# A hybrid RWKV-7 and sparse-attention block on one core: matmuls that nobody reads, the rates in two parts, the norms read back earlier, and new interleaving tables

## The chip, the core and the metric

The kernel runs on one core of a Trainium2 chip. The metric is device time in microseconds of one execution. Engines are named as in the profile: PE is the matmul engine (PEld its weight loads), DVE the vector engine, ACT the scalar engine, POOL the general engine, SP the engine that only issues transfers. Each engine runs its own instructions in the order in which the program lists them, and waits for the others through semaphores.

## The reference

One layer for 512 tokens of width 1024. A normalised, modulated input `h` goes through one projection `w_in` of 6856 columns, which feeds two branches: an RWKV-7 recurrence (eight heads of 64) and attention over keys that an indexer selects. Both are gated, merged and projected out.

```
h = rms_norm(x, norm_w) * (1 + scale) + shift;  p = h @ w_in
w = exp(-DECAY_SCALE * sigmoid(w0 + tanh(wd) @ w_up));  a = sigmoid(a0 + ad @ a_up)
kk = k * k_k / max(norm(k * k_k), 1e-12)
state = state * w_t + (state @ -kk_t) b_t^T + v_t k_t^T;  y_t = state @ r_t
sc = relu(iq . ik);  idx_score = sum_h iw_h * sc_h;  sel = top_k(idx_score, 128)
p = softmax(q . k_sel);  y_b = p @ v_sel
out = x + gate * ((sigmoid(gm_a) * y_a @ w_a_out + sigmoid(gm_b) * y_b @ w_b_out) @ w_o)
```

## The kernel before

All matrices stay on chip in tiles of 128 partitions. Each large projection is made as three matmuls per 128 rows (the high part of one operand times both parts of the other, and the low part times the high one), so that single-precision accuracy is kept. The recurrence is done in eight chunks of 64 tokens: rates per token (`rwkv_rates`), products of keys and rates (`products`), Gram matrices per head and chunk (`gram`), a triangular solve of 32 by 32 blocks on DVE (`solve`), and the chain over the chunks (`chain`). The attention branch has the index scores (`index_pair`, for four query blocks i and four pairs of heads t), the top-128 search (`topk_ops`, alternating MAX8 and MATCH_REPLACE8 on DVE) and the attention itself.

The order of the instructions is written by hand from three generators:

- `main` emits the dependent work (front, index pairs and rates, `prep`, `solve`, eight times `chain`, `attention`), and yields after each step. The n-th yield of a pair (pe, dv) is step n.
- `projections`, the filler, emits the blocks of the big projections, 48 matmuls of 128x512 or 96 of 128x256 to a block, in the order `VRRRVRgqgkvvbbssKQssssss`. It blocks where the next block needs a buffer: the third R waits until the products of head pair 0 are done (`p0`), the first q until `p3`, the first s until the solve is done.
- `dve` holds generators of work for DVE alone: the top-128 search of query blocks 1 to 3, and the group norm.

After step n, `pull(GT[n])` takes about GT[n] us of filler, or as much as there is until it blocks, and `pull_dve(DT[n])` takes that much of `dve`. So the tables GT and DT decide where filler and search stand between the dependent steps, on PE and DVE and, through what the filler needs, on ACT and SP.

A weight half-block comes in by one SP transfer into one of three `wraw` buffers, ACT makes the high part `whi`, DVE the low part `wlo` (L255), and the transfer for the next half-block is queued behind that `wlo`.

`rwkv_rates(t)` makes two matmuls into two banks `ps_yc`, Tanh and Copy on ACT, a scan on DVE, two Exp on ACT that need the scan, a copy on DVE and, last on ACT, the Tanh of the second bank. `index_pair` makes six matmuls into two banks `ps_a` and two Relu on ACT, each followed by one multiply-add on DVE. There are two `ps_a` banks in all, so the next pair's matmuls wait for the Relus of this one.

`norms(t)` writes squared norms (`ds`) to the DRAM tensor `dD` through the ACT queue. `solve` reads them back as `db` and `dR` through the SP queue; PE transposes `dR` (L50), and DVE makes reciprocals of both and scales `PN` with `db`. `PN` itself is read back through the SP queue from `dAB`, which `gram` writes through the POOL queue; the last part of it needs `gram(3)`. After the loop of the solve, its result goes out to DRAM (`dXT`, `dX`) and comes back turned (`X1`, `TT`) before the next matmuls of `solve`.

Of the kernel before, what the change touches and what calls it, by code (L numbers as in the profile page):

```python
# [38 lines left out]
def hybrid_block_kernel(ctx, tc, x, c, norm_w, w_ada, b_ada, w_in, mu, w0, w_up, a0, a_up, k_k, k_a,  # L39
# [6 lines left out]
    def mm(*a, **k):  # L46
        return nc.tensor.matmul(*a, **k)  # L47
# [502 lines left out]
    ETA = {}  # L550

    def rwkv_rates(t):
        Et = T(f"E{t}", [128, 2, S], name="Et")
        E, ta = Et[:, 0], Et[:, 1]
        WX = T("WX", [128, NCH, 65], bufs=4)
        ps, psa = bank("yc"), bank("yc")
        mm(ps, lora[0:64, t * 128:(t + 1) * 128], wdad[0:64, :], start=True, stop=True)
        mm(psa, lora[64:128, t * 128:(t + 1) * 128], wdad[64:128, :], start=True, stop=True)
        act(E, ps, AF.Tanh, scale=0.5, bias=w0h[:, t:t + 1])
        act(E, E, AF.Copy, bias=1.0)  # L560
        L = T("sqL", [128, S], bufs=2, name="L")
        V.tensor_tensor_scan(L, smask, E, 0.0, op0=ALU.mult, op1=ALU.add)
        V.memset(WX[:, :, 0:1], 1.0)
        act(WX[:, :, 1:65], c3(L), AF.Exp, scale=-0.5 * DECAY)
        act(E, L, AF.Exp, scale=0.5 * DECAY)
        V.tensor_copy(wc[:, t, :], WX[:, :, 64])
        act(ta, psa, AF.Tanh, scale=0.5, bias=w0h[:, 4 + t:5 + t])
        ETA[t] = E, ta, WX

    KR, AK, VS, SQ = {}, {}, {}, {}  # L570

    def products(t):
        k, r = KR[t]
# [86 lines left out]
    def prep():  # L660
        for t in range(4):
            yield from need(f"kr{t}")
            yield from need(f"v{t}")
            yield gp(f"need2.{t}")
            yield from products(t)
            if t:
                yield from gram(t - 1)
            else:
                yield gp(f"prod0")
            yield from norms(t)  # L670
            yield from vtrans(t)
            bonus(t)
        V.tensor_copy(bon[64:128, 1], bonn[64:128, 0])
        V.tensor_copy(bon[0:64, 0], bonn[0:64, 1])
        QD['bon'].dma_start(bon[64:128, 0], bonn[0:64, 0])
        QD['bon'].dma_start(bon[0:64, 1], bonn[64:128, 1])
        yield from gram(3)
        done.add("prep")

# [3 lines left out]
    def solve():  # L683
# [1 line left out]
        XT = [XB[:, e] for e in range(2)]  # L685
        X1 = T("E1", [128, NQ, 32], name="X1")
        TTs.extend([T("ar", [128, 16, 64], bufs=2, name="TT") for _ in range(2)])
        db, dR = T("db", [128, 32]), T("dR", [32, 2, 64])
        dzs.append(T("dz", [128, 4, NCH]))
        dz = dzs[0].rearrange("p t c -> p (t c)")  # L690
        for s in range(2):
            QD['db'].dma_start(db[s * 64:s * 64 + 64], dD[:, s].rearrange("t c (b j) -> t (c b) j", j=32))
        for t in range(4):
            QD['db'].dma_start(dR[t * 8:t * 8 + 8], dD[t].rearrange("s c j -> c s j"))
        for e in range(2):
            G.memset(XT[e], 0.0)
            G.memset(XT[e].rearrange("p i j -> p (i j)")[:, e:512:34], 1.0)
# [603 lines left out]
            yield (*gp("need"), 0)  # L1301
        raise RuntimeError(labels)

    def main():
        yield from front()
        RATE = {(1, 1): 0, (1, 3): 1, (2, 2): 2, (3, 0): 3}
        for i in range(1, NT):
            for t in range(4):
                if (i, t) in RATE:
                    rwkv_rates(RATE[i, t])  # L1310
                    yield gp(f"rate.{RATE[i, t]}")
                index_pair(i, t)
                yield gp(f"idx.{i}.{t}")
            dve.append(topk_ops(i))
        yield from prep()
# [11 lines left out]
        yb_split()  # L1327
        done.add("main")

    GT = {0: 2.673, 1: 4.974, 2: 0, 3: 0, 4: 5.748, 5: 0, 6: 0, 7: 5.092, 8: 4.025, 9: 46352.3, 10: 10797.4, 11:  # L1330
# [15 lines left out]
    DT = {0: 0, 1: 1.2, 2: 1.2, 3: 1.2, 4: 0, 5: 0.3, 6: 0.3, 7: 0, 8: 0, 9: 0, 10: 1.5, 11: 0, 12: 0.36, 13: 0.95,  # L1346
# [12 lines left out]
    n = 0  # L1359
    for pe, dv, *w in main():  # L1360
        if w:
# [36 lines left out]
```

## Time and profile before

| | |
|---|---|
| median of three runs | 592.88 us (589.55, 592.88, 593.78) |
| profiled execution | 591.66 us, span 590.0 us |
| PE busy | 537.2 us, 91% of the span |
| DVE busy | 421.2 us, 71% |
| ACT busy | 250.4 us, 42% |
| mean granted clock of PE | 0.957 |

Busy times of matmuls overlap one another, since they are pipelined: what PE does per microsecond is read from the distance between the starts of two matmuls, not from their durations. The clock that PE is granted is either 1.00 or 0.50 in this trace; a mean between them is a mixture of both.

The stages of the span: loads and modulation to about 65 us; projections with the first index pairs to 105; index pairs and rates without filler to 133; products and Gram parts with filler to 192; the last two Gram parts to about 224; the triangular solve to 288; the chain of chunks to 366; attention to about 498; merge and output to 590.

### The profile page before, as it was taken

Reading aid. Unit: us, or ns where it says so; the run is one execution under the profiler, and the core shown is the slowest. Engines: PE = TensorE matmul, PEld = TensorE weight load, DVE = VectorE, ACT = ScalarE, POOL = GpSimd, SP = SyncE. Lnnn points to the kernel's source line nnn. Section 1 sums busy time; section 2 is a strip of 40 time slices with the busy share of each in tenths; the row PEclk is TensorE's granted clock in tenths of the full one; section 3 lists DMA queues with packets and bytes.
Section 4 is the critical chain, followed back from the end, with each engine's and each line's share of the span. In section 5 each row is a group of like instructions: output and inputs, shape, how many; then the busy total and the mean of one; then the engine's idle time right before and its main releaser. Section 6 shows DMA issues by size and latency. Waiting matters only on the chain.

```text
span 590.0 us, 10466 instructions
## 1 busy us (share of the span) xinstructions
PE 537.2 (91%) x4091; PEld 443.8 (75%) x4091; DVE 421.2 (71%) x973; ACT 250.4 (42%) x468; POOL 58.6 (10%) x100
## 2 busy tenths in 40 slices
PE   1699999569999798999789998999998999999997
PEld 0577777327877596998577777987776778998997
DVE  4796667587999665899965566866885637887442
ACT  5833564556344351532434343434535644224110
POOL 7000000002021334020010120220000000000000
PEclk9999999758999797999789999999999999999999
DMA  8992422104645594232473451313221125565522
GB/s 298 318 349 82 117 71 76 33 0 116 177 111 162 144 229 121 72 126 72 142 196 117 170 175 63 89 56 108 73 71 37 37 71 176 147 185 184 168 72 72
DMA packets 80637, 75.00 MB, mean 127 GB/s; under 512 B 15737, under 2 KB 76226, under 8 KB 80588
## 3 DMA queue, kind: packets, MB, share of 16 engines
q1 hardware_dynamic: 74492, 59.86, 34.1%
q0 software_dynamic: 3776, 12.22, 6.9%
q10 hardware_dynamic: 2320, 2.26, 1.2%
q8 instruction: 32, 0.52, 0.4%
q14 instruction: 17, 0.14, 0.1%
HBM read 62.63 MB, written 11.55 MB: 126 GB/s over the span
## 4 chain that ended last, share of the span: by engine, by line
PE 56%; DVE 28%; ACT 6%; DMA 5%; issue 4%; SPq 1%; POOL 1%; DVEq 0%; ACTq 0%
PE ps_pj L47 38%; PE ps_yc L47 6%; PE ps_a L47 5%; DVE wlo L255 4%; PE ps_z L47 3%; DVE bias L527 2%; PE ps_yc L50 2%; DVE m L525 2%; DVE sg L91 2%; PE ps_o L47 2%; DVE pt L724 1%; DVE gacc L91 1%; DMA dAB<-lx 1%; DMA x1b<-in_x_dram 1%; DVE XT L726 1%
## 5 line engine op out<-in xcount | busy, mean ns | idle before, releaser
L47 PE MATMUL ps_pj<-hh,wlo 128*128 128x512 f32 (+1 forms) x304 | 124.3, 409 | 3.7 <-DVE wlo L255 3.7
L47 PE MATMUL ps_pj<-hh,whi 128*128 128x512 f32 (+1 forms) x304 | 124.6, 411 | 1.5 <-ACT hh L88 1.0
L47 PE MATMUL ps_pj<-hl,whi 128*128 128x512 f32 (+1 forms) x304 | 124.2, 409 | 0.8 <-DVE hl L199 0.8
L255 DVE TENSOR_TENSOR wlo<-wraw,whi 128x1024 fp32r<-128x1024 f32 (+2 forms) x80 | 82.9, 1055 | 21.9 <-ACT whi L88 21.8
L88 ACT ACTIVATE whi<-wraw 128x1024 fp32r<-128x1024 f32 (+2 forms) x80 | 71.0, 921 | 25.3 <-DVE xr L1221 19.2
L47 PEld LDWEIGHTS ps_pj<-hh,wlo 128*128 128x128 f32 (+1 forms) x304 | 58.5, 192 | 17.1 <-DVE wlo L255 4.2
L47 PEld LDWEIGHTS ps_pj<-hh,whi 128*128 128x128 f32 (+1 forms) x304 | 58.7, 194 | 16.6 <-ACT hh L88 1.6
L47 PEld LDWEIGHTS ps_pj<-hl,whi 128*128 128x128 f32 (+1 forms) x304 | 58.6, 193 | 15.1 <-DVE hl L199 1.6
L47 PE MATMUL ps_pj<-whi,hh 128*128 128x256 f32 x192 | 54.8, 286 | 0.0
L47 PE MATMUL ps_pj<-whi,hl 128*128 128x256 f32 x192 | 54.4, 283 | 0.0
L47 PE MATMUL ps_pj<-wlo,hh 128*128 128x256 f32 x192 | 54.3, 283 | 0.0
L47 PEld LDWEIGHTS ps_pj<-whi,hh 128*128 128x128 f32 x192 | 36.4, 189 | 0.6
L47 PE MATMUL ps_pj<-whi,mh 128*128 128x256 f32 x128 | 36.4, 284 | 0.0
L47 PEld LDWEIGHTS ps_pj<-whi,hl 128*128 128x128 f32 x192 | 36.2, 189 | 0.0
L47 PEld LDWEIGHTS ps_pj<-wlo,hh 128*128 128x128 f32 x192 | 36.1, 188 | 0.0
L47 PE MATMUL ps_pj<-whi,ml 128*128 128x256 f32 x128 | 36.0, 281 | 0.0
L47 PE MATMUL ps_pj<-wlo,mh 128*128 128x256 f32 x128 | 36.0, 281 | 0.0
L525 DVE MAX8 m<-bias 128x8 f32<-128x256 f32 (+2 forms) x48 | 26.8, 558 | 1.1
L527 DVE MATCH_REPLACE8 bias<-m,bias 128x256 f32<-128x256 f32 (+2 forms) x48 | 26.1, 543 | 0.0
L47 PEld LDWEIGHTS ps_pj<-whi,mh 128*128 128x128 f32 x128 | 24.1, 188 | 0.2 <-ACT gate L88 0.2
L47 PEld LDWEIGHTS ps_pj<-wlo,mh 128*128 128x128 f32 x128 | 24.1, 188 | 0.2 <-issue 0.2
L47 PEld LDWEIGHTS ps_pj<-whi,ml 128*128 128x128 f32 x128 | 24.1, 188 | 0.0
(312 smaller groups left out, 1043.1 us busy)
## 6 DMA issues: line engine op xcount, KB each, us to landing
wraw<-in_w_in_dram SPq DMA_DIRECT2D x44, 512.0 KB
wa<-in_w_ada_dram SPq DMA_DIRECT2D x32, 256.0 KB
lxc<-dLX POOLq DMA_DIRECT2D x8, 768.0 KB, 5.2
wraw<-in_w_in_dram SPq DMA_DIRECT2D x18, 256.0 KB
dLX<-lx SPq DMA_DIRECT2D x8, 512.0 KB
wraw<-in_w_ada_dram SPq DMA_DIRECT2D x8, 512.0 KB
wraw<-in_w_o_dram SPq DMA_DIRECT2D x8, 512.0 KB
wraw<-in_w_a_out_dram SPq DMA_DIRECT2D x16, 128.0 KB
```

The costliest lines, as they stand in the source:

```text
L47: return nc.tensor.matmul(*a, **k)
L50: return nc.tensor.transpose(*a, **k)
L88: A.activation(o, i, func, **kw)
L91: V.scalar_tensor_tensor(o, a, s, b, op0=op0, op1=op1, **kw)
L255: eng.tensor_sub(l_, r_, f(h_))
L525: V.max(out=m8, in_=acc)
L527: V.match_replace(out=acc, in_to_replace=m8, in_values=acc, imm_value=MARK)
L724: V.tensor_mul(pv[e], XT[e][:, a0:, j + 1:], PN[:, j, None, j + 1:].to_broadcast([128, m, n]))
L726: V.tensor_reduce(XT[e][:, (j + 2 - e) // 2:, j], pv[e], axis=AX.X, op=ALU.add)
```

## The change

It has four parts.

1. `warm(count)` emits matmuls of one and the same pair of 128x128 and 128x512 tiles of `hh` into the bank `ps_o`, whose result nothing reads. The table `WT` places 36 of them behind eight steps: 2 behind step 7 (the last index pair of block 1, where filler still runs), 4 behind step 11 (index pair 2.2), 5, 2 and 2 behind 14, 15 and 16 (index pairs 3.0, 3.1, 3.2), 7 behind 20 (the products of head pair 0), 9 behind 40 (first half of the Gram part of head pair 2) and 5 behind 130 (keys of the last head pair in attention). The old `main` becomes `stages`.
2. `rwkv_rates` is a generator. Its first part ends before the two Exp, and the Tanh of the second bank moves into it. The index pair that follows is emitted between the two parts.
3. `db` and `dR` are allocated and read back in `prep`, ahead of `gram(3)`, no longer in `solve`.
4. GT and DT have new values throughout.

```diff
     def rwkv_rates(t):
...
         act(E, E, AF.Copy, bias=1.0)
+        act(ta, psa, AF.Tanh, scale=0.5, bias=w0h[:, 4 + t:5 + t])
         L = T("sqL", [128, S], bufs=2, name="L")
         V.tensor_tensor_scan(L, smask, E, 0.0, op0=ALU.mult, op1=ALU.add)
         V.memset(WX[:, :, 0:1], 1.0)
+        yield
         act(WX[:, :, 1:65], c3(L), AF.Exp, scale=-0.5 * DECAY)
         act(E, L, AF.Exp, scale=0.5 * DECAY)
         V.tensor_copy(wc[:, t, :], WX[:, :, 64])
-        act(ta, psa, AF.Tanh, scale=0.5, bias=w0h[:, 4 + t:5 + t])
         ETA[t] = E, ta, WX
+        yield
...
         QD['bon'].dma_start(bon[0:64, 1], bonn[64:128, 0])
+        dbs.extend([T("db", [128, 32]), T("dR", [32, 2, 64])])
+        for s in range(2):
+            QD['db'].dma_start(dbs[0][s * 64:s * 64 + 64], dD[:, s].rearrange("t c (b j) -> t (c b) j", j=32))
+        for t in range(4):
+            QD['db'].dma_start(dbs[1][t * 8:t * 8 + 8], dD[t].rearrange("s c j -> c s j"))
         yield from gram(3)
...
-        db, dR = T("db", [128, 32]), T("dR", [32, 2, 64])
+        db, dR = dbs
...
-        for s in range(2):
-            QD['db'].dma_start(db[s * 64:s * 64 + 64], dD[:, s].rearrange("t c (b j) -> t (c b) j", j=32))
-        for t in range(4):
-            QD['db'].dma_start(dR[t * 8:t * 8 + 8], dD[t].rearrange("s c j -> c s j"))
...
+    def warm(n):
+
+        if n:
+            ps = bank("o")
+            for _ in range(n):
+                mm(ps, hh[:, 0, 0:128], hh[:, 0, :], start=True, stop=True)
+
     def main():
+        n = 0
+        for y in stages():
+            yield y
+            if len(y) == 2:
+                warm(WT.get(n, 0))
+                n += 1
+
+    WT = {7: 2, 11: 4, 14: 5, 15: 2, 16: 2, 20: 7, 40: 9, 130: 5}
+
+    def stages():
         yield from front()
         RATE = {(1, 1): 0, (1, 3): 1, (2, 2): 2, (3, 0): 3}
         for i in range(1, NT):
             for t in range(4):
-                if (i, t) in RATE:
-                    rwkv_rates(RATE[i, t])
+                rate = rwkv_rates(RATE[i, t]) if (i, t) in RATE else None
+                if rate:
+                    next(rate)
                     yield gp(f"rate.{RATE[i, t]}")
                 index_pair(i, t)
+                if rate:
+                    next(rate)
                 yield gp(f"idx.{i}.{t}")
...
-    GT = {0: 2.673, 1: 4.974, 2: 0, 3: 0, 4: 5.748, 5: 0, 6: 0, 7: 5.092, 8: 4.025, 9: 46352.3, 10: 10797.4, 11:
+    GT = {0: 4.59, 1: 4.327, 2: 0, 3: 0, 4: 13.305, 5: 0, 6: 0, 7: 5.279, 8: 1.036, 9: 148203, 10: 142844, 11:
...
```

How the rows move is shown at two places. The first is the stage of index pairs and rates that has no filler, and there first ACT, before: `Et` and `WX` are tiles of the rates, `L` the result of the scan, `rl` the Relu of an index pair.

```order
L88 ACTIVATE Et_970<-ps_yc_972,w0h_587 128x512
L88 ACTIVATE Et_970<-Et_970 128x512
L88 ACTIVATE WX_971<-L_978 128x8x64
L88 ACTIVATE Et_970<-L_978 128x512
L88 ACTIVATE Et_970<-ps_yc_973,w0h_587 128x512
L88 ACTIVATE rl_1001<-ps_a_993 128x384
L88 ACTIVATE rl_1004<-ps_a_994 128x384
```

And now, at the same place of ACT:

```order
L88 ACTIVATE Et_976<-ps_yc_978,w0h_587 128x512
L88 ACTIVATE Et_976<-Et_976 128x512
L88 ACTIVATE Et_976<-ps_yc_979,w0h_587 128x512
L88 ACTIVATE rl_996<-ps_a_988 128x384
L88 ACTIVATE rl_999<-ps_a_989 128x384
L88 ACTIVATE WX_977<-L_985 128x8x64
L88 ACTIVATE Et_976<-L_985 128x512
```

The two Relus, which the next pair's matmuls wait for, stand ahead of the two Exp that need the scan, no longer behind them. On PE the same stage before, from the matmuls of rate 2 (`lora`) to the norms (`sel`):

```order
L47 MATMUL ps_yc<-wdad,lora 128x512 x2
L47 MATMUL ps_a<-ik,iqs 128x384 x12
L47 MATMUL ps_yc<-wdad,lora 128x512 x2
L47 MATMUL ps_a<-ik,iqs 128x512 x24
L47 MATMUL ps_z<-sq,sel 2x512
```

And now, from the first index pair of that stage to the last:

```order
L47 MATMUL ps_a<-ik,iqs 128x384 x6
L47 MATMUL ps_o<-hh 128x512 x4
L47 MATMUL ps_a<-ik,iqs 128x384 x6
L47 MATMUL ps_yc<-wdad,lora 128x512 x2
L47 MATMUL ps_a<-ik,iqs 128x512 x6
L47 MATMUL ps_o<-hh 128x512 x5
L47 MATMUL ps_a<-ik,iqs 128x512 x6
L47 MATMUL ps_o<-hh 128x512 x2
```

The matmuls into `ps_o` are the unread ones; each group stands ahead of the next index pair, whose matmuls wait for Relus. The second place is the last Gram part and the start of the solve. SP before, from the last transfers of the Gram matrices:

```order
L647 DMA dLX_612<-lx_1826 128x8x128
L656 DMA PN_614<-dAB1_609 8x32x32 x4
L692 DMA db_1964<-dD_613 64x1x32 x2
L694 DMA dR_1965<-dD_613 8x2x64 x4
L321 DMA wraw_1988<-in_w_in_dram 128x4x256
```

And now, from the end of the transfers of the bonus:

```order
L679 DMA bon_621<-bonn_620 64x16
L682 DMA db_1860<-dD_613 64x1x32 x2
L684 DMA dR_1861<-dD_613 8x2x64 x4
L321 DMA wraw_1945<-in_w_in_dram 128x4x256
L321 DMA wraw_2002<-in_w_in_dram 128x4x256
L650 DMA dLX_612<-lx_1868 128x8x128
L650 DMA dLX_612<-lx_1869 128x8x128
L659 DMA PN_614<-dAB1_609 8x32x32 x4
```

The reads of `db` and `dR` were queued behind the last read of `PN`, which waits for `gram(3)`; now they stand ahead of one weight load that was ahead of them, of a second one, of the two stores `dLX` of `gram(3)`, and of that read. DVE before, from the copies of the bonus to the second half of the last Gram part (`lx`; `bias` and `m` are the top-128 search):

```order
L674 COPY bon<-bonn 64x16
L640 TENSOR_TENSOR lx<-ps_yc,mask_167 128x4x2x64
L640 TENSOR_TENSOR lx<-ps_yc,mask_167 128x4x128
L255 TENSOR_TENSOR wlo<-wraw,whi 128x2x2x64 x4
L640 TENSOR_TENSOR lx<-ps_yc,mask_167 128x4x2x64
L640 TENSOR_TENSOR lx<-ps_yc,mask_167 128x4x128
```

And now:

```order
L677 COPY bon<-bonn 64x16
L527 MATCH_REPLACE bias_1040<-m_1848,bias_1040 128x512
L525 MAX m_1891<-bias_1040 128x8
L527 MATCH_REPLACE bias_1040<-m_1891,bias_1040 128x512
L525 MAX m_1894<-bias_1040 128x8
L643 TENSOR_TENSOR lx<-ps_yc,mask_167 128x4x2x64
L643 TENSOR_TENSOR lx<-ps_yc,mask_167 128x4x128
L255 TENSOR_TENSOR wlo<-wraw,whi 128x2x2x64 x4
L527 MATCH_REPLACE bias_1040<-m_1894,bias_1040 128x512
L525 MAX m_1958<-bias_1040 128x8
L527 MATCH_REPLACE bias_1040<-m_1958,bias_1040 128x512
L525 MAX m_1961<-bias_1040 128x8
```

Eight steps of the search stand around the first half of that Gram part. Between the scaling of `PN` and the last step of the solve there were nine such steps on DVE, and now there is none.

More of the change, by code (lines that the diff above doesn't have):

```diff
@@ L566, in rwkv_rates @@
         V.tensor_copy(wc[:, t, :], WX[:, :, 64])
-        act(ta, psa, AF.Tanh, scale=0.5, bias=w0h[:, 4 + t:5 + t])
         ETA[t] = E, ta, WX
-    KR, AK, VS, SQ = {}, {}, {}, {}
+        yield
+    KR, AK, VS, SQ, dbs = {}, {}, {}, {}, []
     def products(t):
@@ L1328, in main @@
         done.add("main")
-    GT = {0: 2.673, 1: 4.974, 2: 0, 3: 0, 4: 5.748, 5: 0, 6: 0, 7: 5.092, 8: 4.025, 9: 46352.3, 10: 10797.4, 11:
[15 rows of a table removed]
-    DT = {0: 0, 1: 1.2, 2: 1.2, 3: 1.2, 4: 0, 5: 0.3, 6: 0.3, 7: 0, 8: 0, 9: 0, 10: 1.5, 11: 0, 12: 0.36, 13: 0.95,
[12 rows of a table removed]
+    GT = {0: 4.59, 1: 4.327, 2: 0, 3: 0, 4: 13.305, 5: 0, 6: 0, 7: 5.279, 8: 1.036, 9: 148203, 10: 142844, 11:
[14 rows of a table added]
+    DT = {0: 2, 1: 0.3, 2: 0, 3: 0.52, 4: 0.08, 5: 0.6, 6: 0.22, 7: 0, 8: 0.38, 9: 0.47, 10: 0, 11: 0, 12: 0.68, 13:
[12 rows of a table added]
     n = 0
```

53 rows, old and new, of tables (DT, GT) are left out of this document.

## Prediction

> **What bounds the kernel now.** I read the page first, then the granted clock over the span, the waits of PE, and the stages in which both come together.
>
> The page gives the span and, in 40 slices of 14.75 us, the clock of PE:
>
> ```profile
> span 590.0 us, 10466 instructions
> ...
> PEclk9999999758999797999789999999999999999999
> ```
>
> The profiled execution took 591.66 us, 1.66 more than its span. The dips stand between slices 8 and 22. With windows on their edges, the columns are length, then busy time of PE, PEld, DVE, ACT and POOL, then clock:
>
> ```profile
> 110.07:130.55 20.48, 13.93 (x52) 7.51 (x52) 17.40 (x42) 12.01 (x22) 0.00 (x0) 0.50 0.00 0
> 133.97:137.38 3.41, 3.41 (x23) 2.39 (x23) 3.20 (x5) 2.56 (x4) 0.00 (x0) 0.50 0.21 49
> 195.41:202.23 6.82, 5.12 (x32) 3.09 (x34) 5.51 (x12) 1.88 (x4) 1.84 (x3) 0.50 0.20 59
> 226.13:232.95 6.82, 5.91 (x14) 4.64 (x15) 4.65 (x9) 1.90 (x3) 2.77 (x5) 0.50 0.51 160
> 287.57:294.39 6.82, 5.54 (x15) 4.47 (x16) 5.64 (x9) 5.75 (x8) 0.00 (x0) 0.50 0.66 211
> 304.63:311.46 6.83, 6.39 (x135) 5.77 (x136) 3.73 (x8) 3.82 (x8) 0.00 (x0) 0.50 0.61 175
> ```
>
> In these six stretches PE works at half speed: its 40.3 busy us there hold some 20 us of work at full clock. What half speed costs is seen in the distance between the starts of two filler matmuls, 0.24 us at full clock and 0.43 at half:
>
> ```profile
> 94.87 0.40 PE L47 MATMUL ps_pj<-hh,wlo 128*128 128x512 f32 x1
> 95.11 0.40 PE L47 MATMUL ps_pj<-hl,whi 128*128 128x512 f32 x1
> ...
> 229.55 0.63 PE L47 MATMUL ps_pj<-hh,wlo 128*128 128x512 f32 x1
> 229.98 0.63 PE L47 MATMUL ps_pj<-hl,whi 128*128 128x512 f32 x1
> ```
>
> Each dip follows or holds a wait of PE. Of the list of waits (total, times, longest) these lie behind the loads:
>
> ```profile
> PE ps_a L47 <- ACT rl L88: 8.2, 4, 4.3
> ...
> PE ps_pj L47 <- DVE wlo L255: 3.7, 1, 3.7
> ...
> PE ps_yc L47 <- DVE lx L640: 3.6, 1, 3.6
> ...
> PE ps_z L47 <- ACT sq L88: 1.4, 1, 1.4
> ```
>
> Four stages, in windows again:
>
> ```profile
> 105.42:132.57 27.15, 15.65 (x63) 8.37 (x62) 21.57 (x49) 15.98 (x28) 0.49 (x1) 0.62 0.00 0
> ...
> 228.40:287.65 59.25, 56.73 (x377) 51.99 (x375) 53.94 (x136) 18.48 (x33) 4.39 (x7) 0.96 0.31 97
> 287.65:301.03 13.38, 12.18 (x48) 9.81 (x48) 8.86 (x13) 7.88 (x12) 1.63 (x3) 0.75 0.68 208
> 366.00:498.00 132.00, 129.56 (x842) 104.44 (x841) 93.35 (x262) 65.86 (x157) 6.62 (x8) 1.00 0.25 74
> ```
>
> The first is the stage of rates and index pairs without filler: nobody is full, a chain over PE, ACT and DVE sets the pace. In the solve both PE (56.73 of 59.25) and DVE (53.94) are nearly full. Attention is PE's, at full clock.
>
> **The change part by part.** *Rates in two parts.* In the first stage ACT and PE do this:
>
> ```profile
> 107.30 0.63 ACT L88 ACTIVATE Et<-Et 128x512 f32<-128x512 f32 x1
> ...
> 110.28 0.67 ACT L88 ACTIVATE Et<-ps_yc,w0h 128x512 f32<-128x512 f32 x1
> 110.85 0.86 ACT L88 ACTIVATE rl<-ps_a 128x384 f32<-128x384 f32 x2
> ...
> 118.77 1.07 ACT L88 ACTIVATE rl<-ps_a 128x512 f32<-128x512 f32 x2
> ```
>
> ```profile
> 95.67 0.80 PE L47 MATMUL ps_a<-ik,iqs 64*128 64x384 f32 x6
> ...
> 119.41 2.13 PE L47 MATMUL ps_a<-ik,iqs 64*128 64x512 f32 x6 [3.34 <-ACT rl L88]
> ...
> 121.81 2.13 PE L47 MATMUL ps_a<-ik,iqs 64*128 64x512 f32 x6 [0.27 <-ACT rl L88]
> ```
>
> After Copy (ends 107.93) ACT waits for the scan, makes two Exp and a Tanh, and only then the Relus at 110.85 that let PE go on. Now Tanh follows Copy at once and the Relus come at 107.93 + 0.67 = 108.60, 2.25 us earlier. The second round (Relus at 118.77) has the same form: 4.5 us in all. The Exp move into the time of DVE's multiply-adds.
>
> *Unread matmuls, 20 in this stage.* If they keep the clock, a pair of 512 columns takes about 0.80 x 512/384 = 1.07 us (an estimate from the 384-column row) rather than 2.13, and the distance of pairs falls from 121.81 - 119.41 = 2.40 to some 1.5, where DVE takes over: three such distances, 2.7 us. At full clock the 20 cost 20 x 0.24 = 4.8 us, in a stage in which PE had 27.15 - 15.65 = 11.5 idle. That cover gone, they cost up to 20 x 0.43 = 8.6.
>
> *Search steps in this stage.* DVE sets a floor. It is busy 21.57 us; the new order has 9 search steps here, formerly 14, each about 0.46 us (MAX8 0.425, the replacement with its load 0.49):
>
> ```profile
> L525 DVE MAX8 m<-bias 128x8 f32<-128x256 f32 x8 | 3.4, 425 | 0.1
> L527 DVE MATCH_REPLACE8 bias<-m,bias 128x256 f32<-128x256 f32 x8 | 3.3, 408 | 0.0
> ...
> L527 DVE MATCH_VALUE_LOAD bias<-m,bias 128x8 f32 x8 | 0.7, 83 | 0.2
> ```
>
> That takes 2.3 off; but index pairs 2.0 and 2.1 now stand closer to the stage, and I put 1.2 us of their multiply-adds into it. Floor 20.5, so of 4.5 + 2.7 at most 6.7 can come. Between 2 (clock not kept, one of the two advances eaten by DVE) and 6.7 I take **5.0**, near the floor, since the floor is what is busy in the row. Step 7's two matmuls stand among filler: **+0.5**.
>
> *Clock at the filler's return.* The stretch 133.97:137.38 is 3.41 busy us at half clock; the 7 matmuls behind step 20 fill the wait before it: **-1.7**, or nothing.
>
> *Nine matmuls in the wait of 3.6 us.* 9 x 0.24 = 2.2 fit in it. If the clock stays, the 5.12 busy us of 195.41:202.23 become 2.6. *Norms read back earlier.* The solve's start, by SP, PE and DVE:
>
> ```profile
> 221.80 1.36 SPq L656 DMA_DIRECT2D PN<-dAB  x2
> ...
> 223.21 1.11 SPq L692 DMA_DIRECT2D db<-dD  x2
> ...
> 224.37 1.50 SPq L694 DMA_DIRECT2D dR<-dD  x4
> ...
> 227.04 0.28 PE L50 MATMUL ps_z<-ident,dR 32*128 32x32 f32 x1 [2.91 <-DMA dR<-dD]
> ...
> 228.40 1.67 DVE L708 TENSOR_TENSOR PN<-PN,db 128x1024 f32<-128x1024 f32 x1
> ```
>
> `dR` is issued only behind `PN`. Ahead of it, its six issues take 1.1 + 1.5 us on SP while the last Gram part is being made; behind them wait one weight load and two stores that have time until the chain. So PE's 2.9 us go, and with them the dip 226.13:232.95, half of 5.91 = 3.0. What is late next is `PN`: issued to 223.16, it can be on chip at about 225 to 226, if `gram(3)` is as early as before. It is not: eight search steps stand around its first half, four of them behind it. They cost 8 x 0.72 = 5.8 us, with rows from the solve's window:
>
> ```profile
> L527 DVE MATCH_REPLACE8 bias<-m,bias 128x512 f32<-128x512 f32 x5 | 3.4, 678 | 0.0
> L525 DVE MAX8 m<-bias 128x8 f32<-128x512 f32 x4 | 2.8, 688 | 0.0
> ```
>
> DVE had idle time there, waiting for `lx` buffers:
>
> ```profile
> 206.01 0.69 DVE L640 TENSOR_TENSOR lx<-ps_yc,mask 128x512 f32<-128x512 f32 x1 [1.92 <-DMA dLX<-lx]
> ...
> 208.86 0.69 DVE L640 TENSOR_TENSOR lx<-ps_yc,mask 128x512 f32<-128x512 f32 x1 [2.16 <-DMA dLX<-lx]
> ```
>
> That covers 4.1 of the 5.8, so `PN` comes 1 to 2 us later, and DVE starts the solve at about 227 instead of 228.4.
>
> *The solve.* Its nine search steps (3.4 + 2.8, with five loads 6.6 us) are gone. DVE keeps 53.94 - 6.6 = 47.3 busy us; with its old idle time, 59.25 - 53.94 = 5.3, it is 52.6. The end moves from 287.65 to between 274.3 and 279.6; PE, which must do the same filler, has lost 2.6 + 2.9 + 3.0 us less before it and can be there at about 278. The 3.7 us wait for `wlo` behind the solve and the dip 287.57:294.39 (half of 5.54) go only in part, since the result's way through DRAM sets that stretch. For everything from 192 to 301 I take **-10**; bounds -2 (search steps come back in front of `PN`, clock lost) and -15 (2.6 + 2.9 + 3.0 + 3.7 + 2.8).
>
> *Chain, attention, merge.* Filler is the same in amount, spread otherwise. In attention PE idles 132.00 - 129.56 = 2.4 us in all, so little can be won; five matmuls stand there where filler is blocked: 0 to 2.2 us. The tables may open or close waits of 2 us. I take **+1**.
>
> Sum: 591.66 + 0.5 - 5.0 - 1.7 - 10 + 1 = 576.5. The median of the three runs, 592.88, is 1.2 above the profiled execution: **577.7**.
>
> **The rivals.**
>
> *DVE takes the gain back.* DVE is nearly full in the solve, and the work taken out is put in front of `PN`. If the idle time doesn't cover it, the solve starts 5.8 us later than the 227 above and PE waits for `wlo` again: the stretch yields about 2 instead of 10, and the time is 585.7. For: 53.94 of 59.25. Against: the two waits for `dLX` of 4.1 us.
>
> *The clock falls all the same.* The clock is low through 110.07:130.55 although PE is busy 13.93 of 20.48, so light work doesn't bring it back; the unread matmuls last 1 us at a time, and the last dip began with this wait only:
>
> ```profile
> 305.07 3.62 PE L47 MATMUL ps_yc<-TT,ZT 32*32 32x32 f32 x128 [1.83 <-DVE ZT L759]
> ```
>
> Then pairs stay at 2.13, the first stage gives 2.5, the return nothing, and the rest 8: 592.88 + 0.5 - 2.5 - 8 + 1 = 583.9. The Trainium skill, "TensorE: Matmul & The Clock Gate", in the table of "Why this matters for your kernels", asks only that no idle gap between bursts is longer than about 3 us; by that rule each group would save the clock, and the sum would stay as above. The row of 1.83 us idle behind 32x32 matmuls speaks against so simple a rule. The same page, Part 1, has the clock return only after about 3.4 us of sustained work; the stretch from 110.07 agrees.
>
> *Slower: the unread matmuls stand in the way.* At half clock five of them last 2.1 us and two 0.9, ahead of index pairs that waited only 0.27 us in the loop of 2.40. That is 1.9 + 2 x 0.6, and 7 x 0.43 - 1.4 = 1.6 from the seven ahead of the norms (the wait for `sq` in the list); with 2.2 in attention and 0.5 at step 7 it is 7.4 us. If in addition the gain of the solve is taken back and ACT's is eaten by DVE, the kernel comes to 592.88 + 7.4 - 2 = 598. It decides when a group lasts longer than the wait it stands in, which needs the low clock.
>
> **How the numbers follow.** The forecast has 0.60, DVE's return 0.18, the falling clock 0.15, the slower case 0.07. The forecast's own bounds are 592.88 + 0.5 - 6.7 - 1.7 - 15 = 570 and 592.88 + 0.5 - 2 - 4 + 2 = 589; the two middle rivals lie inside. The range goes from 569 to 589, the lower end 1 us further out for what the floor of DVE leaves open; it leaves out the slower case and the outer parts of the others. The runs of the kernel before span 0.7%, so 1% (5.9 us) is about what a measurement can tell from no change. Faster than 587 are nearly all of the forecast and most of the two rivals: 0.80; within 1%: 0.14; slower: 0.06.
>
> **What would show it.** Right: the clock at 1.00 from the filler's end to its return; the Relus of the index pair right behind the second Tanh; no wait of PE for `dR`; the stage from the first rate matmuls to the last product 22 us instead of 27; DVE's solve near 50 us instead of 59. Wrong: a dip of the clock in the stage without filler; `PN` scaled later than 228 less the earlier gains; PE waiting for `wlo` in the solve; more than 2.4 us idle on PE in attention.

## The result, and the profile after

The changed kernel takes 573.7 us in the median of its runs, the kernel before 592.9: the ratio is 0.968, with a 95% interval of 0.962 to 0.975. A second series of runs, beside other kernels, gave 573.5 us and 0.969 (0.966 to 0.972). Ratios are of fast runs; of all the kernels below only one, "search out", had a slow one among its five (578.5 us). The prediction, 577.7 with a range of 569 to 589, holds the time. Not all of its reasons hold.

The page of the profiled execution (570.04 us) has these two lines for the span and the clock in 40 slices:

```profile
span 568.3 us, 10555 instructions
...
PEclk9999999998999999999989999999999999999999
```

Two dips are left, in slices 10 and 21. Next, the span by stages, of before and then of after. A window begins with the first rate matmul behind which the filler stands still; the next edges are the filler's return, its last matmul before the Gram parts of head pairs 2 and 3, the scaling of `PN` on DVE, the end of the filler behind the solve, the filler's return at the end of the chain, and the end of the filler in attention. The six stages are called stage A, Gram 0, 1 (the products and the first two Gram parts), Gram 2, 3, the solve, the chain and attention. The columns are length, then busy time of PE, PEld, DVE, ACT and POOL, then clock.

```profile
105.42:133.60 28.18, 16.53 (x71) 9.28 (x71) 22.40 (x51) 16.91 (x30) 0.94 (x1) 0.64 0.00 0
133.60:191.93 58.33, 57.80 (x344) 44.72 (x345) 53.55 (x116) 27.36 (x45) 10.91 (x15) 0.97 0.52 144
191.93:228.40 36.47, 29.87 (x246) 25.29 (x246) 22.72 (x59) 13.65 (x30) 15.91 (x28) 0.88 0.64 165
228.40:300.23 71.83, 68.11 (x418) 61.17 (x417) 62.80 (x147) 25.63 (x42) 6.02 (x10) 0.92 0.37 114
300.23:361.89 61.66, 56.63 (x1102) 46.45 (x1100) 36.07 (x76) 23.94 (x50) 6.40 (x12) 0.94 0.50 158
361.89:493.26 131.37, 128.93 (x845) 104.02 (x844) 94.22 (x280) 65.78 (x161) 6.62 (x8) 1.00 0.22 67
```

```profile
105.71:128.11 22.40, 17.23 (x91) 9.47 (x91) 20.80 (x47) 16.59 (x30) 0.93 (x1) 1.00 0.00 1
128.11:185.81 57.70, 57.62 (x344) 44.73 (x345) 53.84 (x116) 27.98 (x46) 10.88 (x15) 0.97 0.54 150
185.81:219.34 33.53, 32.30 (x267) 27.38 (x267) 27.67 (x72) 13.97 (x30) 13.73 (x24) 1.00 0.69 179
219.34:282.02 62.68, 61.11 (x410) 56.01 (x409) 57.93 (x133) 24.91 (x41) 9.98 (x13) 1.00 0.41 129
282.02:342.70 60.68, 56.36 (x1099) 45.71 (x1096) 38.63 (x83) 23.89 (x50) 6.38 (x12) 0.97 0.50 159
342.70:471.12 128.42, 128.11 (x850) 103.69 (x849) 93.63 (x280) 66.58 (x160) 7.50 (x8) 1.00 0.23 71
```

So stage A gave 5.8 us, Gram 2, 3 gave 2.9, the solve 9.2 and attention 3.0; Gram 0, 1 and the chain gave 0.6 and 1.0. What lies ahead of stage A and behind attention became 0.3 and 0.4 us longer. In stage A the clock is 1.00 instead of 0.64, and DVE is busy 20.80 of 22.40 us.

In the list of waits of PE (total, times, longest) the waits for `dR` and for `wlo` are gone, those for `rl` and `lx` fell from 8.2 and 3.6, and the one for `kr` at the end of stage A grew from 2.1:

```profile
PE ps_z L47 <- DVE kr L91: 3.3, 1, 3.3
...
PE ps_a L47 <- ACT rl L88: 1.1, 2, 0.8
...
PE ps_yc L47 <- DVE lx L643: 0.7, 2, 0.5
```

On ACT, in order of time, the Relus of the index pair follow the second Tanh, which follows the Copy, and the two Exp come behind them. The first Relu starts 108.70 - 107.59 = 1.11 us after the start of the Copy, before it was 110.85 - 107.30 = 3.55:

```profile
107.59 0.63 ACT L88 ACTIVATE Et<-Et 128x512 f32<-128x512 f32 x1
108.13 0.67 ACT L88 ACTIVATE Et<-ps_yc,w0h 128x512 f32<-128x512 f32 x1
108.70 0.86 ACT L88 ACTIVATE rl<-ps_a 128x384 f32<-128x384 f32 x2
109.62 0.63 ACT L88 ACTIVATE WX<-L 128x512 f32<-128x512 f32 x1
```

At the start of the solve DVE now waits for what stood next in the prediction's chain, `PN`:

```profile
216.22 0.35 DVE L711 RECIPROCAL db<-db 128x32 f32<-128x32 f32 x1
219.34 1.23 DVE L712 TENSOR_TENSOR PN<-PN,db 128x1024 f32<-128x1024 f32 x1 [2.77 <-DMA PN<-dAB]
```

### The profile page after: what moved, and what is told of

It reads as the page before. It is cut to its first block, busy times and chain, and to the rows that moved or that the text cites. A ratio compares the mean times of both kernels' runs of the same rounds, so it can differ in the third digit from the quotient of the medians.

```text
span 568.3 us, 10555 instructions
## 1 busy us (share of the span) xinstructions
PE 533.4 (94%) x4127; PEld 441.3 (78%) x4127; DVE 421.2 (74%) x973; ACT 251.3 (44%) x468; POOL 61.7 (11%) x100
## 4 chain that ended last, share of the span: by engine, by line
PE 73%; DVE 15%; ACT 4%; issue 3%; DMA 3%; SPq 2%; DVEq 0%; ACTq 0%
PE ps_pj L47 54%; PE ps_yc L47 5%; PE ps_a L47 5%; PE ps_z L47 4%; PE ps_yc L50 2%; PE ps_o L47 2%; DVE sg L91 2%; DVE bias L527 2%; DVE bias L91 1%; DVE gacc L91 1%; DVE wlo L255 1%; DMA x1b<-in_x_dram 1%; DVE m L525 1%; PE ps_a L50 1%; SPq L659 1%
## 5 line engine op out<-in xcount | busy, mean ns | idle before, releaser
L47 PE MATMUL ps_pj<-hh,whi 128*128 128x512 f32 (+1 forms) x304 | 123.1, 407 | 1.0 <-ACT hh L88 1.0
L47 PE MATMUL ps_pj<-hl,whi 128*128 128x512 f32 (+1 forms) x304 | 122.4, 403 | 0.7 <-DVE hl L199 0.7
L47 PE MATMUL ps_pj<-hh,wlo 128*128 128x512 f32 (+1 forms) x304 | 122.2, 402 | 0.0
L47 PEld LDWEIGHTS ps_pj<-hh,whi 128*128 128x128 f32 (+1 forms) x304 | 57.5, 189 | 14.4 <-ACT hh L88 1.3
L47 PEld LDWEIGHTS ps_pj<-hh,wlo 128*128 128x128 f32 (+1 forms) x304 | 57.6, 190 | 12.5 <-issue 0.2
```

## The experiments

Each run was timed beside the kernel before; the ratio is to that. "Unread" are the matmuls that nobody reads. Each kernel also has a profile, cut at the edges named above; here A begins with the end of the last filler matmul, 0.1 us later. All lengths are in us; "low" is the time between the first loads and the last 2 us for which the granted clock was 0.50.

| kernel | ratio (95%) | A | Gram 0, 1 | Gram 2, 3 | solve | chain | attention | low |
|---|---|---|---|---|---|---|---|---|
| before | 1 | 28.12 | 58.33 | 36.46 | 71.83 | 61.67 | 131.37 | 51.2 |
| changed | 0.968 (0.962 to 0.975) | 22.33 | 57.70 | 33.53 | 62.68 | 60.68 | 128.42 | 6.8 |
| changed, again | 0.969 (0.966 to 0.972) | 23.13 | 58.45 | 34.39 | 63.86 | 64.68 | 128.46 | 20.5 |
| no unread | 0.970 (0.966 to 0.974) | 22.35 | 57.68 | 35.30 | 62.54 | 61.88 | 129.90 | 34.1 |
| unread late | 0.968 (0.965 to 0.971) | 22.37 | 57.70 | 33.94 | 64.17 | 62.21 | 128.43 | 27.3 |
| rates whole | 0.980 (0.976 to 0.984) | 28.81 | 57.73 | 36.34 | 62.48 | 63.71 | 128.43 | 30.7 |
| norms late | 0.976 (0.973 to 0.979) | 22.34 | 57.71 | 36.70 | 66.24 | 63.87 | 128.40 | 20.5 |
| search back | 0.980 (0.976 to 0.984) | 22.37 | 57.68 | 32.48 | 65.15 | 64.26 | 131.68 | 10.2 |
| search back, 2 | 0.971 (0.968 to 0.973) | 22.35 | 57.71 | 32.67 | 65.20 | 62.39 | 128.42 | 13.7 |
| old tables | 0.990 (0.986 to 0.993) | 26.21 | 59.09 | 33.27 | 68.97 | 62.73 | 131.37 | 30.7 |
| tables only | 0.989 (0.987 to 0.992) | 30.17 | 58.39 | 38.01 | 65.68 | 60.65 | 129.95 | 44.4 |
| kr early | 0.970 (0.967 to 0.973) | 22.37 | 57.69 | 34.42 | 63.77 | 62.32 | 128.41 | 13.7 |
| search out | 0.964 (0.961 to 0.966) | 20.93 | 58.05 | 35.23 | 64.02 | 59.20 | 128.42 | 6.8 |
| search out, late | 0.969 (0.966 to 0.972) | 23.10 | 58.82 | 33.98 | 63.95 | 62.08 | 128.41 | 34.1 |

The changed kernel itself was run again, as the mark for the runs that followed:

> The changed kernel itself, timed again beside the next three as their mark: 572 to 575, ratio 0.964 to 0.970.

It came as expected. Its two profiles show how far one profile carries: 0.1 us in attention, 0.8 in A, 2.0 in the sum of Gram 2, 3 and the solve, 4.0 in the chain. The 0.8 in A are all at its end: the last matmuls of the norms start 21.51 us behind the first rate matmul both times, and in the second profile they ran at half clock.

**Without the unread matmuls.**

```diff
-    WT = {7: 2, 11: 4, 14: 5, 15: 2, 16: 2, 20: 7, 40: 9, 130: 5}
+    WT = {}
```

> The changed kernel without its 36 unread matmuls; the rest as it is. Stage A is the stage of rates and index pairs from the filler's stop to its return: 28.1 us before, 22.4 changed. If the unread matmuls keep the clock (the forecast), the clock falls to 0.50 within some 4 us of the filler's stop, a pair of 512 columns takes about 2.1 us again, stage A is 25 to 26 us (the earlier Relus stay), a second dip comes at the Gram part of head pair 2, and the time is 578 to 583. If the tables and the split rates did it all (rival), stage A stays within 1 us of 22.4 or gets shorter and the time is 571 to 575.

The ratio is 0.970, against 0.968 and 0.969 with them. The forecast's theory had the clock right, though the fall came 9.0 us after the filler's end (104.52) and not within 4, and the time wrong. The window of stage A, and the pairs in it by time on PE:

```profile
104.45:126.87 22.42, 14.76 (x72) 7.38 (x71) 20.82 (x47) 16.47 (x30) 0.94 (x1) 0.77 0.01 1
113.53:123.77 10.24, 7.89 (x35) 3.34 (x31) 9.45 (x21) 6.27 (x11) 0.00 (x0) 0.50 0.00 0
```

```profile
115.08 2.13 PE L47 MATMUL ps_a<-ik,iqs 64*128 64x512 f32 x6 [0.72 <-ACT rl L88]
117.48 2.13 PE L47 MATMUL ps_a<-ik,iqs 64*128 64x512 f32 x6 [0.27 <-ACT rl L88]
120.97 1.87 PE L47 MATMUL ps_z<-sq,sel 128*2 128x512 f32 x2 [1.36 <-ACT sq L88]
```

The clock falls for 10.24 us and a pair takes 2.13 us again, as forecast, and the stage is as long as before within 0.02 us. DVE is busy 20.82 of it, as it was with them. The half clock lies wholly beside DVE's work.

The other places: without the nine, Gram 2, 3 is 0.9 to 1.8 us longer, but the solve behind it makes that good (35.30 + 62.54 = 97.84, between 96.21 and 98.25 of the changed kernel). Without the five, attention is 1.5 us longer, with a clock of 0.50 from 434 to 438 us, which begins 2 us behind a wait of PE of 1.2 us for `qs`; the five stand in that wait.

**Only the unread matmuls of the later places.**

```diff
-    WT = {7: 2, 11: 4, 14: 5, 15: 2, 16: 2, 20: 7, 40: 9, 130: 5}
+    WT = {40: 9, 130: 5}
```

> The changed kernel with 14 of the 36 unread matmuls: the nine at the Gram part of head pair 2 and the five in attention stay, the 22 in and ahead of stage A go. New theory: DVE sets stage A, so the clock may fall there at no cost: stage A 22.4 us within 0.5 at a clock near 0.6, the time that of the changed kernel within 1.5 us. Rival: the clock of stage A is worth the forecast's 2.7 us once the rest is in step: stage A 24 us or more, 575 to 578.

A is 22.37 us, the ratio 0.968. The 22 unread matmuls in and ahead of stage A are worth nothing there. Nor do they always keep the clock: with all of them it fell in stage A in the two kernels below that have the rates whole (111.69 to 118.52 us) or the old tables (112.72 to 119.54), at waits of PE for Relus of 4.0 and 1.7 us.

**The rates in one piece.**

```diff
         act(E, E, AF.Copy, bias=1.0)
-        act(ta, psa, AF.Tanh, scale=0.5, bias=w0h[:, 4 + t:5 + t])
...
-        yield
         act(WX[:, :, 1:65], c3(L), AF.Exp, scale=-0.5 * DECAY)
         act(E, L, AF.Exp, scale=0.5 * DECAY)
         V.tensor_copy(wc[:, t, :], WX[:, :, 64])
+        act(ta, psa, AF.Tanh, scale=0.5, bias=w0h[:, 4 + t:5 + t])
...
-                if rate:
-                    next(rate)
```

> The changed kernel with the rates in one piece again: the Relus stand behind the scan, the two Exp and the second Tanh. Forecast's term: they come 2.25 us later in each of two rounds, stage A is 25 to 27 us instead of 22.4, the time 576 to 579. Rival: DVE sets stage A (20.8 us busy of 22.4), and the later Relus cost less than 1 us: 573 to 575.

A is 28.81 us, 6.5 more, longer than either theory had it, and the time is 581.3 us, the ratio 0.980: (0.980 - 0.969) x 592 = 6.5 us. In the list of waits PE's wait for `rl` is back:

```profile
PE ps_a L47 <- ACT rl L88: 5.6, 2, 4.0
```

And the window of stage A:

```profile
106.28:135.17 28.89, 20.09 (x92) 12.09 (x91) 22.10 (x50) 16.81 (x30) 0.93 (x1) 0.82 0.01 2
```

DVE is busy 22.10 of 28.89 us: it stands still for lack of Relus and of what the Exp make. The clock is 0.82, so the 6.5 us may hold a part that the clock lost; no run separates it. Without the split, the tables and the unread matmuls bring nothing in stage A.

**The norms read back in the solve.**

```diff
-        dbs.extend([T("db", [128, 32]), T("dR", [32, 2, 64])])
-        for s in range(2):
-            QD['db'].dma_start(dbs[0][s * 64:s * 64 + 64], dD[:, s].rearrange("t c (b j) -> t (c b) j", j=32))
...
         yield from gram(3)
...
-        db, dR = dbs
+        db, dR = T("db", [128, 32]), T("dR", [32, 2, 64])
...
+        for s in range(2):
+            QD['db'].dma_start(db[s * 64:s * 64 + 64], dD[:, s].rearrange("t c (b j) -> t (c b) j", j=32))
...
```

> The changed kernel with db and dR read back in the solve again, behind PN on SP's queue. Forecast's term: PE waits some 2.9 us for dR and loses up to 3.0 more to the clock: 577 to 580. Rival: PN, not dR, lets DVE start the solve, and PE makes up the wait in the filler of the solve: less than 1 us, 573 to 575.

The median is 578.9 us, as expected; the ratio is 0.976, 0.007 x 592 = 4 us more. The wait for `dR` is back and twice as long as in the kernel before:

```profile
PE ps_z L50 <- DMA dR<-dD: 5.8, 1, 5.8
```

Gram 2, 3 and the solve together are 102.94 us against 96.21 and 98.25: 4.7 to 6.7. The forecast's 5.9 lies in that.

**Eight search steps back into the solve, twice.**

```diff
     DT = {
...
-        44: 3.07, 45: 2.33,
+        44: 0, 45: 0,
...
-        49: 0, 50: 0, 61: 0, 63: 0, 64: 0, 66: 0, 69: 0, 72: 0, 73: 0,
+        49: 0.82, 50: 0.21, 61: 1.33, 63: 0.22, 64: 0.22, 66: 0.61, 69: 0.43, 72: 0.22, 73: 1,
...
```

The first time the remainder that DVE's table carries from step to step was 0.14 us off behind the solve, so that DVE's steps stood otherwise in the chain and in attention. The second time `84: 1.06` instead of 1.2 put that right.

> The changed kernel with eight search steps of 512 columns taken from the first half of gram(3) and put back into the loop of the solve. Forecast's term: they cost 8 x 0.72 = 5.8 us on DVE in a solve in which DVE has hardly any slack; some 1 to 2 us come back at the start of the solve, which is then earlier: the stretch from the scaling of PN to the end of the filler behind the solve grows from 62.7 to 66 to 68 us, the time is 576 to 579. Rival: PE's filler sets the end of the solve and DVE's steps fit beside it: 572 to 575.

> The eight search steps back in the loop of the solve, as in the first such run, but with one table value 0.14 lower so that DVE's order from the chain on is that of the changed kernel again. If the attention's 3.3 us longer stage in the first run came from the shifted order there, it is gone (128.4 us), and what is left is the price of the steps in the solve: 575 to 579. Rival: the steps in the solve cost all of the 7.5: attention 131 us or more, 580 to 582.

The medians are 581.0 and 574.9 us, the ratios 0.980 and 0.971. With the order behind the solve the same as in the changed kernel, the eight steps in the solve cost 0.971 - 0.969, some 1 us, and the intervals overlap. Gram 2, 3 got shorter, the solve longer, and their sum is 32.67 + 65.20 = 97.87 us, between the 96.21 and 98.25 of the changed kernel. The forecast had them at 2.5 to 5.5 us of time.

The other 5 us of the first run went with the shifted order. Attention shows 3.3 of them, 131.68 instead of 128.42 us, with two waits of PE in it that the changed kernel doesn't have; where the rest went the profiles don't settle:

```profile
PE ps_yc L50 <- DVE qn L914: 1.8, 1, 1.8
PE ps_pj L47 <- ACT sq L88: 1.1, 1, 1.1
```

**The parts without the tables, and the tables without the parts.** The first kernel is the changed one with GT and DT of before, the second the one before with the new GT and DT. The edit of the first, against the changed kernel, is below; the second makes the same edit to the kernel before, the other way round:

```diff
-    GT = {0: 4.59, 1: 4.327, 2: 0, 3: 0, 4: 13.305,
+    GT = {0: 2.673, 1: 4.974, 2: 0, 3: 0, 4: 5.748,
...
-    DT = {0: 2, 1: 0.3, 2: 0, 3: 0.52, 4: 0.08,
+    DT = {0: 0, 1: 1.2, 2: 1.2, 3: 1.2, 4: 0,
...
```

> The changed kernel with the GT and DT of the kernel before, so the unread matmuls, the rates in two parts and the early norms alone. By the forecast's sum the code parts bring 5 in stage A and 5.9 of dR with its dip, less what PN still holds up, and the solve keeps its nine search steps (71.8 us to the end of the filler behind it): 580 to 584. Rival one: without the tables the parts bring little, since the search steps of the old order stand elsewhere: 587 or more. Rival two: the tables bring nothing: 573 to 576.

> The kernel before with the new GT and DT alone: rates in one piece, norms read back in the solve, no unread matmul. If the parts add up as they came off the changed kernel (7.8 for the rates, 5.4 for the norms, 0 to 1 for the unread matmuls), 573.5 + 13 to 14 = 586 to 588, so the tables alone bring 5 where they brought 12.5 on top of the other parts. Rival: tables and parts are independent, and the tables alone bring the 12.5 that were missing without them: 578 to 581. Second rival: written for the other order, they bring nothing or cost: 590 or more.

The medians are 586.0 us and 585.0 us: the parts alone bring less than the forecast's sum for them (580 to 584), the tables alone a little more than what the sum of the parts left for them. In ratios, the parts alone bring 1.0%, 6 us, the tables alone 1.1%, 6.5 us, both together 3.1%, 18 us. Their waits of PE, first of the parts without the tables, then of the tables without the parts:

```profile
PE ps_pj L47 <- DVE wlo L255: 4.4, 1, 4.4
...
PE ps_a L47 <- ACT rl L88: 2.4, 2, 1.7
```

```profile
PE ps_a L47 <- ACT rl L88: 9.7, 4, 5.5
PE ps_z L50 <- DMA dR<-dD: 5.9, 1, 5.9
```

Without the tables the wait for `wlo` stays, and the solve has 68.97 us; without the parts the waits for `rl` and `dR` get longer than they were (8.2 and 2.9). So each half runs into waits that the other half takes away. That this makes up the 18 - 12.5 = 5.5 us is a reading of the lists; no run was made to test it. Attention is 131.37 with the old tables, with the five unread matmuls and without, 129.95 with the new ones and 128.4 with the new ones and the five.

**Five search steps from behind steps 19 to 21 to behind steps 24 and 26.**

```diff
     DT = {
...
-        19: 0.6, 20: 0.6, 21: 0.5, 24: 0, 26: 0.5,
+        19: 0, 20: 0, 21: 0, 24: 1, 26: 1.2,
...
```

> The changed kernel with the five search steps behind steps 19 to 21, which stand on DVE ahead of the normalised keys that PE waits for at the end of stage A, put behind steps 24 and 26, where filler runs. If DVE sets stage A, it shortens by 1.5 to 2.3 us (five steps of 0.45 to 0.49) to about 20.3, the wait for kr falls from 3.4 to about 1.3 us, and the time falls by 1 to 2.3 us unless DVE is late with wlo in the stage behind, where it is busy 53.8 of 57.7 us. Rival: ACT or PE sets the end of stage A: no change, within 0.7 us.

A is 22.37 us, the time 574.7: no change. The expectation was wrong on the place: in DVE's row of the changed kernel these steps follow the multiply-add that writes `kr`, they do not lead it:

```profile
126.33 0.75 DVE L91 SCALAR_TENSOR_TENSOR kr<-ar,P,kb 128x512 f32<-128x512 f32 x1
127.00 0.08 DVE L527 MATCH_VALUE_LOAD bias<-m,bias 128x8 f32 x1
```

So this run says nothing on what DVE does to stage A; the next two do.

**Seven search instructions out of stage A, with and without the unread matmuls there.** The first also has six unread matmuls between the two halves of the solve's result; the second has the same DT, and of the unread matmuls only the 14 of the later places (`{40: 9, 130: 5}`).

```diff
-    WT = {7: 2, 11: 4, 14: 5, 15: 2, 16: 2, 20: 7, 40: 9, 130: 5}
+    WT = {7: 2, 11: 4, 14: 5, 15: 2, 16: 2, 20: 7, 40: 9, 130: 5, 84: 6}
...
     DT = {
...
-        12: 0.68, 14: 0.3, 15: 1.04, 16: 0.6, 24: 0, 26: 0.5,
+        12: 0, 14: 0, 15: 0, 16: 0, 24: 1.2, 26: 1.9,
...
```

> The changed kernel with the seven search instructions (four MAX8, three replacements) that stand on DVE between the index pairs of stage A, ahead of the normalised keys, moved behind steps 24 and 26, and six unread matmuls more behind the first half of the solve's result, where PE waits 1.6 us and a dip of the clock follows. If DVE sets stage A: 4 x 0.43 + 3 x 0.49 = 3.2 us less on DVE, stage A 19.2 to 20.5 us instead of 22.35. If the six keep the clock at the start of the chain, that stage stays at or below 60.7 us, where five of six profiles of the changed kernel and its kin had 61.9 to 64.7. Together 568 to 571. Rival: PE or ACT sets stage A as soon as DVE is lighter: 21.5 or more there, 572 to 574.

> The same move of the seven search instructions, with only the unread matmuls at the Gram part of head pair 2 and in attention (14). With DVE lighter in stage A the low clock may be felt there: pairs of 512 columns 2.40 apart, stage A 20.5 to 22.4 us against 19.2 to 20.5 with the unread matmuls, and 570 to 573. Rival: DVE still hides the clock, stage A equal within 0.4 us with and without them.

Stage A in windows, first with the unread matmuls, then without:

```profile
105.97:126.97 21.00, 17.06 (x92) 9.47 (x91) 18.33 (x36) 16.37 (x30) 0.94 (x1) 1.00 0.00 1
```

```profile
105.36:128.53 23.17, 16.64 (x72) 9.11 (x71) 19.09 (x38) 17.28 (x32) 0.93 (x1) 0.61 0.04 9
```

With both the search away and the clock kept, A is 20.93 us, 1.4 less than in the changed kernel (the expectation's 19.2 to 20.5 was too low); with the search away alone it is 23.10 (20.5 to 22.4 was expected), no better than in the changed kernel, and the time is 573.3 us. The pairs show why: 2.40 us apart at the half clock, 2.04 and 2.01 at the full one. At the half clock DVE, now lighter, waits for the Relus of every pair:

```profile
113.52 2.13 PE L47 MATMUL ps_a<-ik,iqs 64*128 64x512 f32 x6 [0.66 <-ACT rl L88]
115.92 2.13 PE L47 MATMUL ps_a<-ik,iqs 64*128 64x512 f32 x6 [0.27 <-ACT rl L88]
...
118.30 1.61 DVE L91 SCALAR_TENSOR_TENSOR bias<-rl,iw,bias 128x512 f32<-128x512 f32 x2 [0.79 <-ACT rl L88]
```

```profile
114.14 1.44 PE L47 MATMUL ps_a<-ik,iqs 64*128 64x512 f32 x6
115.52 0.73 PE L47 MATMUL ps_o<-hh 128*128 128x512 f32 x2
116.18 1.42 PE L47 MATMUL ps_a<-ik,iqs 64*128 64x512 f32 x6
...
118.19 1.32 PE L47 MATMUL ps_a<-ik,iqs 64*128 64x512 f32 x6
```

Two limits of nearly the same length lie beside each other in this stage: DVE with the search steps, and PE with its Relus at half clock. The norms' matmul behind the last pair starts 16.5 us after the first rate matmul under either limit (122.22 - 105.71 in the changed kernel, 121.81 - 105.36 = 16.45 without search and unread matmuls) and 15.3 when both are lifted (121.25 - 105.97). The multiply-add that writes `kr`, which the end of the stage waits for, ends 21.4 and 21.3 us behind the first rate matmul under one limit, and 20.0 when both are lifted. Lifting one shows nothing. The 0.8 us by which 23.10 is longer than 22.33 lie behind `kr`, as in the second profile of the changed kernel: the norms' last matmuls at half clock.

The six unread matmuls in the solve's result stand in the wait for `ZT`, of 1.6 us; the clock stays at 1.00 there, and the chain has 59.20 us, the least of all profiles. The first kernel's ratio, 0.964 (0.961 to 0.966), is the best of all: (0.969 - 0.964) x 592 = 3 us less than the changed kernel's second series, which ran beside other kernels, and the intervals touch. How the 3 us divide between stage A and the chain, the single profiles do not settle.

## Why the prediction was right or wrong

- **The sum.** 577.7 was forecast, 573.7 measured. The profiled execution went from 591.66 to 570.04, by 21.6 where the sum had 15.2. Stretch by stretch, with the forecast's term behind: +0.3 ahead of stage A (+0.5), -5.8 in stage A (-5.0), -0.6 at the filler's return (-1.7), -12.1 from Gram 2, 3 to the end of the solve (-10), -3.5 behind it (+1). The median fell by 19.2 only, since the profiled execution is the fastest of its four; that the forecast came within 4.0 is in part luck, as some terms are right for reasons that the runs don't bear out. The upper bound of 589 takes off 2 and 4, where the two bounds that the text names are 2 and 2: with them it is 591.
- **Rates in two parts.** Right in mechanism: the Relus come right behind the second Tanh. The term was 4.5 for ACT, with 2.7 more for the clock and a floor of 20.5 by DVE. Measured: the split is worth 6.5 us with the new tables, a lost clock included; with the old ones the split and the unread matmuls together give 1.9 (26.21 against 28.12). There DVE has 14 search instructions ahead of `kr`, in the changed kernel nine, as counted in the forecast. The floor was sized well: DVE is busy 20.80.
- **Unread matmuls in stage A.** With them the clock stayed at 1.00 in stage A in the changed kernel's first profile and up to its last 2 us in the second, as forecast, and that is worth nothing. The step "if they keep the clock ... three such distances, 2.7 us" fails, because the half clock lay beside DVE. The prediction took 5.0 of 7.2 for this very floor, but cut the sum and not the term. With DVE lighter the clock is worth 2.2 us (23.10 against 20.93), 0.8 of them in the norms' last matmuls. The term was mis-sized too: a pair of 512 columns lasts 1.3 to 1.45 us at full clock, where 384 columns gave an estimate of 1.07, and the pairs are 2.0 us apart, not 1.5, with the clock kept and the search away.
- **Clock at the filler's return, -1.7, or nothing.** It was nothing. The seven matmuls stand ahead of the norms; the wait behind them, for `kr`, was 2.1 us and is now 3.35, and the dip stayed:

```profile
128.23:131.64 3.41, 3.41 (x14) 2.28 (x15) 3.20 (x10) 2.26 (x4) 0.00 (x0) 0.50 0.29 66
```

- **Nine matmuls in the wait of 3.6 us.** The dip went, as forecast, and came back in the kernel without them. The 2.6 us show as 0.9 to 1.8 in Gram 2, 3 and not at all in the sum with the solve.
- **Norms read back earlier.** Right: the wait for `dR` and its dip are gone, `PN` is what is late next (2.77 us on DVE), and taking the part back costs 4 us of time, 4.7 to 6.7 in the profile. Forecast 5.9. A new wait of PE for ACT (`th`), of 1.6 and 1.8 us in the two profiles of the changed kernel, stands 7 us behind the scaling of `PN`; the second profile has a dip of 3.41 us there, the first has none.
- **The solve.** The time was nearly right (12.1 us for Gram 2, 3 and the solve, where 10 were forecast from 192 to 301), the step is wrong: that "its nine search steps" are gone is worth about 1 us of time, by the eight put back. On DVE the solve did get shorter, from 59.3 us to 53.5 and 54.7 in the two profiles (near 50 was forecast), and it is 56.1 with the eight back. What the new tables took away was the wait for `wlo` of 3.7 us: it is 4.4 with the old tables and early norms, and 1.3 and 0.7 in the two kernels with the new ones and eight search steps in the solve; the new tables without the parts have no such wait at all. So the eight steps don't explain it. GT, the filler's places, and the rest of DT are left; which entry does it was not tried, and the cause stays open there.
- **Chain, attention, merge, +1.** Wrong in sign: the chain gave 1.0, within its spread of 4.0, attention 3.0, and the end took 0.4. Of the 3.0 in attention the tables give 1.4 and the five unread matmuls 1.5. That PE had 2.4 us idle there was read as little to win; nearly all of it was won.
- **The rivals.** DVE did not take the gain back, and no run shows a group of unread matmuls that costs time, though with the old tables five of them, at half clock, last from 114.90 to 117.33 us and hold up the pair behind them while DVE is busy with other work. "The clock falls all the same" came true at two places (the filler's return and the start of the chain); where the clock does fall in stage A, without the unread matmuls, it costs nothing: that rival's price was wrong too.

## What to carry to other kernels

Before paying for a clock, look which engine sets the pace of the stage in which it is low: 10 us at half clock were free here, because another engine was busy 93% of the stage. Where two limits are equally long, an experiment that lifts one shows nothing; lift both, and then each. A hand-written order and the code that it orders belong together: here each half alone was worth a third of the whole, and ran into waits that the other half removes.

## What the runs showed of the hardware

Between the first loads and the last 2 us the stretches of low clock last 3.41 us or a multiple of it in every profile, and they do not lie at the same place in two executions of one kernel: the two profiles of the changed kernel have 6.8 and 20.5 us of it, and differ by 6.4 us of span (568.3 and 574.7), of which 4.0 are in the chain. The Trainium skill, "TensorE: Matmul & The Clock Gate", Part 1, describes a free-running window of 3413 ns; these lengths agree.

Long idle time is not needed for a dip. At the start of the chain PE waits 1.61 us between matmuls of 32x32, which are short and many, and the clock is 0.50 right behind:

```profile
282.39 2.21 PE L47 MATMUL ps_yc<-X,NO 32*32 32x32 f32 x128
286.21 1.20 PE L47 MATMUL ps_yc<-TT,ZT 32*32 32x32 f32 x64 [1.61 <-DVE ZT L763]
```

```profile
288.65:292.07 3.42, 3.42 (x19) 2.58 (x13) 0.94 (x3) 2.79 (x6) 0.00 (x0) 0.50 0.54 184
```

The gap from 284.60 (282.39 + 2.21) to 286.21 is 1.61 us. In the one profile that has six matmuls of 128x512 in this gap the clock stayed at 1.00; each of the thirteen others has a dip there, 3 to 7 us behind the filler's end:

```profile
286.78 1.66 PE L47 MATMUL ps_o<-hh 128*128 128x512 f32 x6
288.46 1.20 PE L47 MATMUL ps_yc<-TT,ZT 32*32 32x32 f32 x64
```

The same page of the Trainium skill, "Why this matters for your kernels", asks that no idle gap be longer than about 3 us. Here gaps of half that, among small matmuls, were enough; whether it is the rows of the array that small matmuls leave unused, no run here separates from the gap itself.
